# A prefix log-sum-exp over 4096 rows: another order at the end, another split into tiles, and other overflow checks

## The chip, the cores and the metric

The kernel runs on one core of one Trainium2 chip. The metric is the device time of one launch in microseconds. A core has engines that run side by side and wait for each other through semaphores: PE (TensorE, matrix products into PSUM), DVE (VectorE), ACT (ScalarE, here Exp and Ln), POOL (GpSimd) and SP (SyncE, which here only issues transfers), and 16 DMA engines that move data between HBM and the on-chip SBUF.

## The reference

For each of four batches and each of 4128 columns, a running log-sum-exp over 4096 rows:

```
B, S, D = 4, 4096, 4128
out[:, 0, :] = x[:, 0, :]
for t in range(1, S):
    mx = np.maximum(out[:, t - 1, :], x[:, t, :])
    out[:, t, :] = mx + np.log(np.exp(out[:, t - 1, :] - mx) + np.exp(x[:, t, :] - mx))
```

Input and output are float32, 270.5 MB each. Since out[t] is the log of the sum of exp(x) over rows 0 to t, the kernel computes exp, a prefix sum over rows, and a log, without the maximum. Whether that was safe for the data is looked at on the way (the probes, below); if it was not, a slow general routine runs afterwards.

## The kernel before

**Tiles.** A batch's 4096 rows are cut into tiles of 2 or 3 times 128 rows. Partition p of a tile holds r consecutive rows (r is 2 or 3), each of 4128 columns. Every batch is split as 2,3,3,3,2,3,3,3,2,3,3,2, twelve tiles and 48 in all, counted from 0 here. There are four buffers: three of three rows (pool `x3`) and one of two (pool `x2`), which every fourth tile takes. A tile's columns are worked in three chunks of 1376.

**A chunk**, as class `Chunk` has it:

- `exp` (ACT, L92): Exp of all r rows in place.
- `sums` (DVE, L103 for three rows, L105 always): sums within a partition, so that `z` holds each partition's total for partitions 0 to 126. Partition 127 of `z` still holds what the chunk of the same columns in the tile before left there, that is the running total so far.
- `head` (PE, L113): a product of a triangular matrix with `z`, which gives each partition the sum of all rows before it; `carried` also adds the running total, `below` is for a batch's first tile. The result lies in PSUM tile `pt`, of which there are two.
- `add` (DVE, L121 and L122): adds `pt` to all rows but the last, and then writes the last row's sum to `z`, which is the next tile's running total.
- `log` (ACT, L135 and L136): Ln of the rows, the last one from `z`, into the tile.

After its three chunks a tile is stored (SP, L83). Loads are issued at L80. All transfers are issued by SP, in program order.

**Probes.** In a batch's first tile `sums` also takes, per chunk, the minimum over the first row (DVE, L99). In a batch's last tile `add` also takes, per chunk, the sum over columns of the last 32 partitions of `z` (DVE, L128). At the end these are compared with `SMALL` and `LARGE`, and a product on PE makes one flag of them.

**Order.** The kernel switches the scheduler off, so each engine runs its instructions in the order in which the program writes them. One loop runs over all chunks, 144 of them. In each turn it writes the Exp of the chunk two ahead, the sums of the next chunk, then the add and the log of this one, at a tile's end its store and the next load, and the matmul of the next chunk. For the chunks where the one two ahead lies in the last tile, or where there is none, the branch `late` writes the Exp and the sums behind the add and the log instead. The load of tile t+3 stands behind the store of tile t, and waits for the store of tile t-1, whose buffer it takes.

The lines of that branch:

```
        late = far is None or far.t is steps[-1]
        if not late:
            far.exp()
            nxt.sums()
        k.add()
        k.log()
        if late:
            if far:
                far.exp()
            if nxt:
                nxt.sums()
```

Of the kernel before, what the change touches and what calls it, by code (L numbers as in the profile page):

```python
# [7 lines left out]
FP32 = mybir.dt.float32  # L8
I32 = mybir.dt.int32
ACT = mybir.ActivationFunctionType  # L10
ALU = mybir.AluOpType
AX = mybir.AxisListType
P = 128
MM = 512
NC = 3
SMALL = 2.0 ** -63
LARGE = 2.0 ** 62


@with_exitstack  # L20
def kernel(
    ctx: ExitStack,
    tc: tile.TileContext,
    x: bass.AP,
    out: bass.AP,
):
    nc = tc.nc
    B, S, D = x.shape
# [12 lines left out]

    below = consts.tile([P, P], FP32, name="below")
    nc.gpsimd.memset(below, 1.0)  # L43
    nc.gpsimd.affine_select(  # L44
        out=below, in_=below, pattern=[[1, P]], compare_op=ALU.is_ge,
        fill=0.0, base=-1, channel_multiplier=-1,
    )

    carried = consts.tile([P, P], FP32, name="carried")
    nc.gpsimd.affine_select(  # L50
        out=carried, in_=below, pattern=[[0, P]], compare_op=ALU.not_equal,
        fill=1.0, base=-(P - 1), channel_multiplier=1,
    )
    ones = consts.tile([P, 1], FP32, name="ones")
    nc.gpsimd.memset(ones, 1.0)

    probe = consts.tile([P, 2, B * NC], FP32, name="probe")
    nc.gpsimd.memset(probe, 1.0)

    z = [zpool.tile([P, CH], FP32, name=f"z{c}") for c in range(NC)]  # L60
    for t in z:
        nc.gpsimd.memset(t, 0.0)  # L62

    ctx_sched = tc.manual_schedule()
    ctx_sched.__enter__()

    class Step:
        def __init__(self, b, row, r, pool, last):
            self.b, self.row, self.r, self.pool = b, row, r, pool
            self.first, self.last = row == 0, last  # L70

        def dram(self, t):
            rows = t[self.b, self.row:self.row + P * self.r, :]
            return rows.rearrange("(p j) d -> p j d", j=self.r)

        def load(self):
            rows = 2 if self.pool is x2 else 3
            full = self.pool.tile([P, rows, D], FP32, name="xt")
            self.xt = full[:, :self.r, :]
            nc.sync.dma_start(out=self.xt, in_=self.dram(x))  # L80

        def store(self):
            nc.sync.dma_start(out=self.dram(out), in_=self.xt)  # L83

    class Chunk:
        def __init__(self, step, c):
            self.t, self.c, self.z = step, c, z[c]
            self.cols = slice(c * CH, (c + 1) * CH)

        def exp(self):  # L90
            e = self.t.xt[:, :, self.cols]
            nc.scalar.activation(e, e, ACT.Exp)  # L92

        def sums(self):
            t, r = self.t, self.t.r
            e = [t.xt[:, j, self.cols] for j in range(r)]
            if t.first:
                k = t.b * NC + self.c
                nc.vector.tensor_reduce(  # L99
                    out=probe[0:1, 1, k:k + 1], in_=e[0][0:1], op=ALU.min, axis=AX.X,  # L100
                )
            if r == 3:
                nc.vector.tensor_tensor(out=e[1], in0=e[0], in1=e[1], op=ALU.add)  # L103
            n = P - 1
            nc.vector.tensor_tensor(  # L105
                out=self.z[0:n], in0=e[r - 2][0:n], in1=e[r - 1][0:n], op=ALU.add,
            )

        def head(self):
            pt = self.pt = ppool.tile([P, CH], FP32, name="pt")  # L110
            w = below if self.t.first else carried
            for a, b in cuts:
                nc.tensor.matmul(  # L113
                    pt[:, a:b], lhsT=w, rhs=self.z[:, a:b], start=True, stop=True,
                )

        def add(self):
            t, r = self.t, self.t.r
            e = t.xt[:, 0:r - 1, self.cols]
            base = self.pt.unsqueeze(1).to_broadcast([P, r - 1, CH])  # L120
            nc.vector.tensor_tensor(out=e, in0=base, in1=e, op=ALU.add)  # L121
            nc.vector.tensor_tensor(  # L122
                out=self.z, in0=t.xt[:, r - 2, self.cols], in1=t.xt[:, r - 1, self.cols],
                op=ALU.add,
            )
            if t.last:
                k = t.b * NC + self.c
                nc.vector.tensor_reduce(  # L128
                    out=probe[96:P, 0, k:k + 1], in_=self.z[96:P], op=ALU.add, axis=AX.X,
                )  # L130

        def log(self):
            t, r = self.t, self.t.r
            e = t.xt[:, 0:r - 1, self.cols]
            nc.scalar.activation(e, e, ACT.Ln)  # L135
            nc.scalar.activation(t.xt[:, r - 1, self.cols], self.z, ACT.Ln)  # L136

    steps = []
    for b in range(B):
        n = S // P  # L140
        parts = []
        while n:
            r = min(2 if len(parts) % 4 == 0 else 3, n)
            if n - r == 1:
                r = 2
            parts.append(r)
            n -= r
        assert len(parts) % 4 == 0 and min(parts) > 1
        row = 0
        for i, r in enumerate(parts):  # L150
            steps.append(Step(b, row, r, x3 if i % 4 else x2, i + 1 == len(parts)))
            row += P * r
        assert row == S

    chunks = [Chunk(s, c) for s in steps for c in range(NC)]
    bufs, ahead, stored = 4, 3, 0
    for s in steps[:bufs]:
        s.load()
    chunks[0].exp()
    chunks[1].exp()  # L160
    chunks[0].sums()
    chunks[0].head()
    n = len(chunks)
    for g, k in enumerate(chunks):
        nxt = chunks[g + 1] if g + 1 < n else None
        far = chunks[g + 2] if g + 2 < n else None
        late = far is None or far.t is steps[-1]
        if not late:
            far.exp()
            nxt.sums()  # L170
        k.add()
        k.log()
        if late:
            if far:
                far.exp()
            if nxt:
                nxt.sums()
        if k.c == NC - 1:
            k.t.store()
            if bufs <= stored + ahead < len(steps):  # L180
                steps[stored + ahead].load()
            stored += 1
        if nxt:
            nxt.head()


    bad = consts.tile([P, 2, B * NC], FP32, name="bad")
    nc.vector.tensor_scalar(
        out=bad[:, 0, :], in0=probe[:, 0, :], scalar1=LARGE, scalar2=None, op0=ALU.is_le,
    )  # L190
    nc.vector.tensor_scalar(
        out=bad[:, 1, :], in0=probe[:, 1, :], scalar1=SMALL, scalar2=None, op0=ALU.is_ge,
    )
    low = consts.tile([P, 1], FP32, name="low")
    nc.vector.tensor_reduce(  # L195
        out=low, in_=bad.rearrange("p a k -> p (a k)"), op=ALU.min, axis=AX.X,
    )
    good = fpool.tile([1, 1], FP32, name="good")
    nc.tensor.matmul(good, lhsT=low, rhs=ones, start=True, stop=True)  # L199
    flag = consts.tile([1, 1], I32, name="flag")  # L200
    nc.vector.tensor_scalar(  # L201
        out=flag, in0=good, scalar1=float(P), scalar2=None, op0=ALU.is_lt,
    )
    ctx_sched.__exit__(None, None, None)

    wrong = nc.values_load(flag[0:1, 0:1], min_val=0, max_val=1)
    with tc.If(wrong > 0):
        _general(tc, x, out)
# [62 lines left out]
```

## Time and profile before

| What | Value |
|---|---|
| median of three runs | 1296.6 us (1295.03 to 1298.33) |
| the profiled execution: its own time | 1293.67 us |
| its span in the trace | 1291.9 us |
| PE busy | 605.4 us (47%) |
| DVE busy | 996.0 us (77%) |
| ACT busy | 937.3 us (73%) |
| POOL busy | 4.6 us, all of it in the first 5.2 us |
| bytes moved, HBM read and written | 270.53 MB each way, 419 GB/s over the span |
| Exp, L92, three rows or two | 3.63 us or 2.48 us |
| sums, L103 and L105 | 1.59 us each |
| add, L121, three rows or two | 3.02 us or 1.58 us |
| carry, L122 | 1.59 us |
| Ln, L135, three rows or two, and L136 | 2.50 us or 1.35 us, and 1.33 us |
| probes L99 and L128, twelve of each | 1.57 us and 1.58 us |
| load from issue to landing, three rows, two rows | 38.9 us, 33.2 us |
| store from issue to landing, three rows, two rows | 23.8 us, 26.4 us |

The span runs from the first instruction to the end of the last; the time of a run is a little longer. All durations are of the one profiled execution. A transfer is issued long before its bytes move where the queue holds others ahead of it, so its time from issue to landing is mostly waiting in the queue. Matmuls overlap each other, so the busy time of PE is not a sum of work. The chain that ended last is followed back from the last instruction, and says nothing of the transfers that lay beside it.

### The profile page before, as it was taken

What the parts mean: (1) busy time and instruction counts of PE and PEld (TensorE: products, weight loads), DVE (VectorE), ACT (ScalarE), POOL (GpSimd) and SP (SyncE); (2) the same over time, 40 slices, a digit from 0 to 9 for tenths busy, and PEclk for the clock granted to TensorE, in tenths of its full rate; (3) what the DMA queues carried; (4) which work ended last, traced back from release to release, by engine and by line L of the source; (5) the groups of instructions that cost most, each with busy time, mean ns of one, the idle gap of its engine ahead of it and who ended that gap; (6) DMA issues with size and microseconds to landing.
All of it is one profiled execution on the core that took longest, in us unless ns stands there. A gap on an engine that the chain in (4) does not pass through costs nothing. (4 is left out here: it accounts for less than half of the span.)

```text
span 1291.9 us, 3364 instructions
## 1 busy us (share of the span) xinstructions
PE 605.4 (47%) x866; PEld 236.8 (18%) x866; DVE 996.0 (77%) x556; ACT 937.3 (73%) x433; POOL 4.6 (0%) x12
## 2 busy tenths in 40 slices
PE   2554356345555335545534534535534553463432
PEld 1221122112122112112211211211211221121110
DVE  4996798679689579669968957957968976895763
ACT  4996687678589669569669957866858866895761
POOL 1000000000000000000000000000000000000000
PEclk9766666667567667666766766766776666676566
DMA  9999999999999999999999999999999999999964
GB/s 402 423 413 428 433 429 432 436 430 404 438 433 427 439 427 431 435 430 420 423 425 435 439 428 439 428 438 426 415 429 429 435 434 432 434 437 429 433 279 180
DMA packets 13843, 541.28 MB, mean 419 GB/s; under 512 B 1536, under 2 KB 1536, under 8 KB 1536
## 3 DMA queue, kind: packets, MB, share of 16 engines
q1 hardware_dynamic: 13824, 541.07, 97.6%
q8 instruction: 7, 0.11, 0.0%
q14 instruction: 12, 0.10, 0.0%
HBM read 270.53 MB, written 270.53 MB: 419 GB/s over the span
## 5 line engine op out<-in xcount | busy, mean ns | idle before, releaser
L113 PE MATMUL pt<-z,carried 128*128 128x512 f32 (+1 forms) x792 | 557.9, 867 | 613.2 <-DVE z L105 613.2
L92 ACT ACTIVATE xt<-xt 128x4128 f32<-128x4128 f32 (+1 forms) x144 | 467.7, 3249 | 240.3 <-DMA xt<-in_x_dram 240.3
L113 PEld LDWEIGHTS pt<-z,carried 128*128 128x128 f32 x792 | 218.0, 293 | 952.4 <-issue 952.4
L121 DVE TENSOR_TENSOR xt<-pt,xt 128x2752 f32<-128x2752 f32 (+1 forms) x144 | 365.6, 2539 | 20.9 <-PE pt L113 20.9
L135 ACT ACTIVATE xt<-xt 128x2752 f32<-128x2752 f32 (+1 forms) x144 | 303.8, 2109 | 100.3 <-DVE z L122 99.7
L103 DVE TENSOR_TENSOR xt<-xt 128x1376 f32<-128x1376 f32 x96 | 152.3, 1587 | 216.4 <-ACT xt L92 216.3
L105 DVE TENSOR_TENSOR z<-xt 127x1376 f32<-127x1376 f32 x144 | 228.9, 1590 | 17.8 <-ACT xt L92 13.8
L122 DVE TENSOR_TENSOR z<-xt 128x1376 f32<-128x1376 f32 x144 | 229.3, 1593 | 4.9
L136 ACT ACTIVATE xt<-z 128x1376 f32<-128x1376 f32 x144 | 192.0, 1333 | 0.0
L113 PE MATMUL pt<-z,below 128*128 128x512 f32 (+1 forms) x72 | 47.3, 817 | 54.4 <-DVE z L105 54.4
L99 DVE TENSOR_REDUCE probe<-xt 1x1 f32<-1x1376 f32 x12 | 18.9, 1571 | 21.8 <-ACT xt L92 21.7
L113 PEld LDWEIGHTS pt<-z,below 128*128 128x128 f32 x72 | 18.7, 276 | 83.1 <-issue 82.9
L128 DVE TENSOR_REDUCE probe<-z 32x1 f32<-32x1376 f32 x12 | 19.0, 1581 | 0.4
L62 POOL MEMSET z<- 128x1376 f32 x3 | 3.7, 1245 | 0.0
L199 PE MATMUL good<-ones,low 128*1 128x1 f32 x2 | 0.2, 164 | 5.4 <-DVE low L195 5.4
L33 ACT ACT_TABLE_LOAD x1 | 1.3, 1283 | 0.8 <-PEq L255 0.8
L199 PEld LDWEIGHTS good<-ones,low 128*1 128x1 f32 x2 | 0.1, 82 | 6.0 <-DVE low L195 6.0
L201 DVE TENSOR_SCALAR flag<-good 1x1 int32<-1x1 f32 x1 | 0.1, 147 | 0.3 <-PE good L199 0.3
L44 POOL TENSOR_SCALAR_AFFINE_SELECT below<-below 128x128 f32<-128x128 f32 x1 | 0.3, 292 | 0.0
L50 POOL TENSOR_SCALAR_AFFINE_SELECT carried<-below 128x128 f32<-128x128 f32 x1 | 0.3, 292 | 0.0
L195 DVE TENSOR_REDUCE low<-bad 128x1 f32<-128x24 f32 x1 | 0.2, 179 | 0.0
L43 POOL MEMSET below<- 128x128 f32 x1 | 0.2, 204 | 0.3 <-POOLq L255 0.3
(8 smaller groups left out, 1.0 us busy)
## 6 DMA issues: line engine op xcount, KB each, us to landing
xt<-in_x_dram SPq DMA_DIRECT2D x32, 6192.0 KB, 38.9
out_dram<-xt SPq DMA_DIRECT2D x32, 6192.0 KB, 23.8
xt<-in_x_dram SPq DMA_DIRECT2D x16, 4128.0 KB, 33.2
out_dram<-xt SPq DMA_DIRECT2D x16, 4128.0 KB, 26.4
```

The source lines that it names most:

```text
L33: nc.scalar.preload_act_table_set("natural_log_exp_and_others")
L62: nc.gpsimd.memset(t, 0.0)
L92: nc.scalar.activation(e, e, ACT.Exp)
L99: nc.vector.tensor_reduce(out=probe[0:1, 1, k:k + 1], in_=e[0][0:1], op=ALU.min, axis=AX.X,)
L103: nc.vector.tensor_tensor(out=e[1], in0=e[0], in1=e[1], op=ALU.add)
L105: nc.vector.tensor_tensor(out=self.z[0:n], in0=e[r - 2][0:n], in1=e[r - 1][0:n], op=ALU.add,)
L113: nc.tensor.matmul(pt[:, a:b], lhsT=w, rhs=self.z[:, a:b], start=True, stop=True,)
L121: nc.vector.tensor_tensor(out=e, in0=base, in1=e, op=ALU.add)
L122: nc.vector.tensor_tensor(out=self.z, in0=t.xt[:, r - 2, self.cols], in1=t.xt[:, r - 1, self.cols], op=ALU.add,)
L128: nc.vector.tensor_reduce(out=probe[96:P, 0, k:k + 1], in_=self.z[96:P], op=ALU.add, axis=AX.X,)
L135: nc.scalar.activation(e, e, ACT.Ln)
L136: nc.scalar.activation(t.xt[:, r - 1, self.cols], self.z, ACT.Ln)
```

## The change

Five things are changed together.

- The branch `late` is gone. Each engine now has a list of its own (`act`, `vec`, `pe` and `moves`), written out for all tiles in one pattern. The pattern is the one that the loop before had away from its end: on ACT, Exp runs two chunks ahead; on DVE, the sums of the next chunk come before the add of this one. A loop then writes the lists out, each as far as what it needs has been written.
- The split into tiles is given as lists: `usual` for the first three batches, `final` for the last one, which now has thirteen tiles, 49 in all. Tiles 45 to 48 have 3, 3, 3 and 2 rows.
- The load of the last tile is issued directly behind the load before it, and so ahead of the store of tile 45 and not behind it.
- The look at a batch's first row is done by GpSimd: a comparison with `SMALL` into `ample` and a product into `least`, per chunk, written behind the chunk's Exp. One DVE minimum over `least` is left for the end.
- The look at a batch's last rows is no instruction of its own: the addition that writes `z` is done by `tensor_tensor_reduce`, which also writes the sum over columns, now for all 128 partitions.

```
--- before.py
+++ after.py
-    probe = consts.tile([P, 2, B * NC], FP32, name="probe")
+    probe = consts.tile([P, B * NC], FP32, name="probe")
     nc.gpsimd.memset(probe, 1.0)
+    least = consts.tile([1, CH], FP32, name="least")
+    nc.gpsimd.memset(least, 1.0)
+    ample = consts.tile([1, CH], FP32, name="ample")
...
         def exp(self):
-            e = self.t.xt[:, :, self.cols]
+            t = self.t
+            e = t.xt[:, :, self.cols]
             nc.scalar.activation(e, e, ACT.Exp)
+            if t.first:
+                nc.gpsimd.tensor_scalar(
+                    out=ample, in0=t.xt[0:1, 0, self.cols], scalar1=SMALL, scalar2=None,
+                    op0=ALU.is_ge,
+                )
+                nc.gpsimd.tensor_tensor(out=least, in0=least, in1=ample, op=ALU.mult)
 
         def sums(self):
-            t, r = self.t, self.t.r
-            e = [t.xt[:, j, self.cols] for j in range(r)]
-            if t.first:
-                k = t.b * NC + self.c
-                nc.vector.tensor_reduce(
-                    out=probe[0:1, 1, k:k + 1], in_=e[0][0:1], op=ALU.min, axis=AX.X,
-                )
...
         def add(self):
...
-            nc.vector.tensor_tensor(
-                out=self.z, in0=t.xt[:, r - 2, self.cols], in1=t.xt[:, r - 1, self.cols],
-                op=ALU.add,
-            )
+            ends = (t.xt[:, r - 2, self.cols], t.xt[:, r - 1, self.cols])
             if t.last:
-                k = t.b * NC + self.c
-                nc.vector.tensor_reduce(
-                    out=probe[96:P, 0, k:k + 1], in_=self.z[96:P], op=ALU.add, axis=AX.X,
+                nc.vector.tensor_tensor_reduce(
+                    out=self.z, in0=ends[0], in1=ends[1], scale=1.0, scalar=0.0,
+                    op0=ALU.add, op1=ALU.add, accum_out=probe[:, k:k + 1],
                 )
+            else:
+                nc.vector.tensor_tensor(out=self.z, in0=ends[0], in1=ends[1], op=ALU.add)
...
+    usual = [2, 3, 3, 3, 2, 3, 2, 3, 2, 3, 3, 3]
+    final = [2, 3, 2, 3, 2, 2, 3, 2, 2, 3, 3, 3, 2]
...
+    moves = [("load", t) for t in range(SLOTS)]
+    ahead = SLOTS
+    for t in range(n):
+        moves.append(("store", t))
+        if t and ahead < n:
+            moves.append(("load", ahead))
+            ahead += 1
+            if ahead == n - 1:
+                moves.append(("load", ahead))
+                ahead += 1
...
+    act.append(("exp", 0, 0))
+    act.append(("exp", 0, 1))
+    vec.append(("sums", 0, 0))
+    for t in range(n):
+        act += [("exp", t, 2), ("log", t, 0), ("exp", t + 1, 0), ("log", t, 1),
+                ("exp", t + 1, 1), ("log", t, 2)]
+        vec += [("sums", t, 1), ("add", t, 0), ("sums", t, 2), ("add", t, 1),
+                ("sums", t + 1, 0), ("add", t, 2)]
+        pe += [("head", t, c) for c in range(NC)]
...
+    fits = consts.tile([P, B * NC + 1], FP32, name="fits")
+    nc.vector.memset(fits[:, B * NC:], 1.0)
+    nc.vector.tensor_reduce(
+        out=fits[0:1, B * NC:], in_=least, op=ALU.min, axis=AX.X,
+    )
```

Of the old code, the loop over chunks with its branch `late` and the rule that split the batches are taken out; the two comparisons with `SMALL` and `LARGE` at the end become one with `LARGE`, over `probe`.

More of the change, by code (lines that the diff above doesn't have):

```diff
@@ L15 @@
 NC = 3
+SLOTS = 4
 SMALL = 2.0 ** -63
@@ L90, in exp @@
         def exp(self):
-            e = self.t.xt[:, :, self.cols]
+            t = self.t
+            e = t.xt[:, :, self.cols]
             nc.scalar.activation(e, e, ACT.Exp)
-        def sums(self):
-            t, r = self.t, self.t.r
-            e = [t.xt[:, j, self.cols] for j in range(r)]
-            if t.first:
-                k = t.b * NC + self.c
-                nc.vector.tensor_reduce(
-                    out=probe[0:1, 1, k:k + 1], in_=e[0][0:1], op=ALU.min, axis=AX.X,
-                )
+            if t.first:
[4 more added lines that the diff above has]
+                nc.gpsimd.tensor_tensor(out=least, in0=least, in1=ample, op=ALU.mult)
+        def sums(self):
+            r = self.t.r
+            e = [self.t.xt[:, j, self.cols] for j in range(r)]
             if r == 3:
@@ L118, in add @@
             t, r = self.t, self.t.r
+            k = t.b * NC + self.c
             e = t.xt[:, 0:r - 1, self.cols]
@@ L136, in log @@
             nc.scalar.activation(t.xt[:, r - 1, self.cols], self.z, ACT.Ln)
+    usual = [2, 3, 3, 3, 2, 3, 2, 3, 2, 3, 3, 3]
+    final = [2, 3, 2, 3, 2, 2, 3, 2, 2, 3, 3, 3, 2]
     steps = []
     for b in range(B):
[L140 to L148, printed above, removed]
+        parts = final if b == B - 1 else usual
@@ L149 @@
         row = 0
         for i, r in enumerate(parts):
-            steps.append(Step(b, row, r, x3 if i % 4 else x2, i + 1 == len(parts)))
+            if row == S:
+                break
+            pool = x3 if len(steps) % SLOTS else x2
+            steps.append(Step(b, row, r, pool, row + P * r == S))
             row += P * r
         assert row == S
[L155 to L184, printed above, removed]
@@ L187 @@
-    bad = consts.tile([P, 2, B * NC], FP32, name="bad")
-    nc.vector.tensor_scalar(
-        out=bad[:, 0, :], in0=probe[:, 0, :], scalar1=LARGE, scalar2=None, op0=ALU.is_le,
+    for s in steps:
+        s.chunks = [Chunk(s, c) for c in range(NC)]
+    n = len(steps)
+    moves = [("load", t) for t in range(SLOTS)]
[8 more added lines that the diff above has]
+                ahead += 1
@@ new lines @@
+    lists = {"move": moves, "act": [], "vec": [], "pe": []}
+    act, vec, pe = lists["act"], lists["vec"], lists["pe"]
+    act.append(("exp", 0, 0))
[7 more added lines that the diff above has]
+        pe += [("head", t, c) for c in range(NC)]
@@ new lines, in needs @@
+    def needs(what, t, c=None):
+        if what == "load":
+            return [("store", t - SLOTS)]
+        if what == "store":
+            return [("log", t, c) for c in range(NC)]
+        return {
+            "exp": [("load", t)],
+            "sums": [("exp", t, c), ("log", t - 1, c)],
+            "head": [("sums", t, c), ("add", t - 1, c)],
+            "add": [("head", t, c)],
+            "log": [("add", t, c)],
+        }[what]
+    done, at = set(), {e: 0 for e in lists}
+    while any(at[e] < len(l) for e, l in lists.items()):
+        before = len(done), sum(at.values())
+        for e, l in lists.items():
+            while at[e] < len(l):
+                op = l[at[e]]
+                if op[1] < n:
+                    if any(0 <= d[1] and d not in done for d in needs(*op)):
+                        break
+                    done.add(op)
+                    of = steps[op[1]]
+                    getattr(of if len(op) == 2 else of.chunks[op[2]], op[0])()
+                at[e] += 1
+        assert before != (len(done), sum(at.values()))
@@ L190 @@
+    fits = consts.tile([P, B * NC + 1], FP32, name="fits")
+    nc.vector.memset(fits[:, B * NC:], 1.0)
+    nc.vector.tensor_reduce(
+        out=fits[0:1, B * NC:], in_=least, op=ALU.min, axis=AX.X,
     )
     nc.vector.tensor_scalar(
-        out=bad[:, 1, :], in0=probe[:, 1, :], scalar1=SMALL, scalar2=None, op0=ALU.is_ge,
+        out=fits[:, :B * NC], in0=probe, scalar1=LARGE, scalar2=None, op0=ALU.is_le,
     )
     low = consts.tile([P, 1], FP32, name="low")
-    nc.vector.tensor_reduce(
-        out=low, in_=bad.rearrange("p a k -> p (a k)"), op=ALU.min, axis=AX.X,
-    )
+    nc.vector.tensor_reduce(out=low, in_=fits, op=ALU.min, axis=AX.X)
```

## The prediction

> **What bounds the kernel now.** I read the slices of the page first, then its DMA queues, then windows over the end, then the issues of SP, and the chain that ended last only after these.
>
> ```profile
> DMA  9999999999999999999999999999999999999964
> GB/s 402 423 413 428 433 429 432 436 430 404 438 433 427 439 427 431 435 430 420 423 425 435 439 428 439 428 438 426 415 429 429 435 434 432 434 437 429 433 279 180
> q1 hardware_dynamic: 13824, 541.07, 97.6%
> ```
>
> The reader sees that the transfers fill 38 of 40 slices and that only the last two sag. DVE is busy for 77% of the span and ACT for 73%: neither sets the time in the middle, they run ahead of the loads (ACT waited 240.3 us for loads in the table of waits). So the time is bytes over rate, plus whatever the queue stands dry. Windows of ten microseconds over the end (columns: stretch, length, busy time and count of PE, PEld, DVE, ACT, POOL, granted clock, DMA share, GB/s):
>
> ```profile
> 1230.00:1240.00 10.00, 4.93 (x6) 1.86 (x6) 4.85 (x4) 6.35 (x4) 0.00 (x0) 0.54 0.78 337
> 1240.00:1250.00 10.00, 3.86 (x5) 1.83 (x6) 5.96 (x3) 5.42 (x3) 0.00 (x0) 0.50 0.19 79
> 1250.00:1260.00 10.00, 3.36 (x5) 1.20 (x5) 6.36 (x4) 5.68 (x4) 0.00 (x0) 0.67 0.92 396
> 1260.00:1270.00 10.00, 3.36 (x6) 1.39 (x5) 6.36 (x4) 2.59 (x2) 0.00 (x0) 0.67 0.37 159
> 1270.00:1280.00 10.00, 2.94 (x7) 1.00 (x6) 5.34 (x7) 2.59 (x2) 0.00 (x0) 0.67 0.12 53
> 1280.00:1290.00 10.00, 0.00 (x0) 0.00 (x0) 0.00 (x0) 0.00 (x0) 0.00 (x0) 0.50 0.87 371
> ```
>
> What is missing to a share of 1 in these six is 2.2 + 8.1 + 0.8 + 6.3 + 8.8 + 1.3 = 27.5 us. That is the idle that a change of the end can win. Why it is there is seen in the issues of the last three stores (tiles 45, 46, 47, counted from 0) and in one load that landed before them:
>
> ```profile
> 1207.25 3.64 ACT L92 ACTIVATE xt<-xt 128x4128 f32<-128x4128 f32 x1 [7.69 <-DMA xt<-in_x_dram]
> 1222.56 0.33 SPq L83 DMA_DIRECT2D out_dram<-xt  x1
> 1248.34 0.33 SPq L83 DMA_DIRECT2D out_dram<-xt  x1
> 1278.72 0.33 SPq L83 DMA_DIRECT2D out_dram<-xt  x1
> ```
>
> A tile of three rows is 6192 KB, which at the steady 433 GB/s is 14.6 us (estimate), one of two rows 9.8 us. Store 45 is through 15 us after 1222.56, store 46 is issued 26 us after it and store 47 another 30 us later: twice the queue waits for compute. The chain says on what:
>
> ```profile
> 1257.70 4.42 PE pt L113 x6
> 1262.12 0.02 issue
> 1262.14 1.60 DVE xt L121
> 1263.75 0.02 issue
> 1263.77 1.60 DVE z L122
> 1265.38 0.02 issue
> 1265.40 1.58 DVE probe L128
> 1266.98 0.03 issue
> 1267.01 1.60 DVE z L105
> 1268.62 0.14 issue
> 1268.75 4.02 PE pt L113 x6
> ```
>
> In the last tile each chunk runs alone: matmul, add, carry, probe, then the sums of the next chunk, and only then its matmul: 11 us a chunk, 33 us for a tile whose DVE work, spread as in the middle, takes half of that.
>
> **The change, part by part.**
>
> Order kept to the end. The branch `late` goes, so the sums of the next chunk stand before the add of this one in the last tile too, and its matmul lies beside that add. Cost per chunk from the rows: exp 3.63 or 2.48 (three or two rows), sums 3.2 or 1.6, add with carry 3.02 + 1.59 = 4.6 or 1.6 + 1.6 = 3.2, Ln pair 3.8 or 2.7, matmul 4 to 4.9. Check on the middle: from the landing of a load to the issue of the store of the tile before lie exp, sums, add and Ln pair, 3.6 + 3.2 + 4.6 + 3.8 = 15.2; the lines above show 1222.56 - 1207.25 = 15.3.
>
> New end, 3,3,3,2 (tiles 45 to 48), and load 48 ahead of store 45. Put T at the landing of load 47. Behind it the one queue then holds load 48 (9.8), stores 45, 46 and 47 (14.6 each) and store 48 (9.8): it is busy to T + 63.4 if each is issued in time. Store 46 is issued at T + 15.3; the queue needs it at T + 24.4. From there DVE sets the pace, its last add of tile 46 being done at T + 11.4: sums 14.6, add 19.2, sums 22.4, add 27.0, sums of tile 48 28.6, add 33.2, Ln pair: store 47 at T + 37.1, needed at T + 39.0. Tile 48: sums 34.8, add 38.0, sums 39.6, matmul of chunk 1 from 34.9 to 39.9, add 43.1, matmul of chunk 2 to 44.8, add 48.0, Ln pair: store 48 at T + 50.7, needed at T + 53.6. So nothing runs dry, with 2 to 3 us to spare, and all 27.5 us go. An issue takes one to two microseconds to become bytes (load 0: issue 0.81, share 0.72 in the first five), so the two tight stores may leave 0 to 4 us; I take 1. The shares are means over 16 engines and the last one counts; the share falls from 0.92 to 0.18 at 1238 and to 0 at 1240, so I add 2 (0 to 3).
>
> Thirteen tiles. The old split 3,3,2 under the new order would leave store 46 due at 15.3 + 21.8 = 37 us after the landing of load 46, with 9.8 + 9.8 + 14.6 = 34 us queued: some 4 us dry. The new split is worth that, inside the 27.5. The bytes are the same; two more transfers, three more chunks on PE and nine more ACT instructions lie under DMA.
>
> Load 48 before store 45. SP stands at this load until store 44 has landed, and store 45 is behind it. Store 44 lands 9.8 us after load 46, store 45 has its data only at 15.3: nothing waits. The transfer merely trades places with a store: 0.
>
> Split in the middle. Between the landing of load t+1 and the end of load t+2 the queue holds store t-1 and load t+2. The old split has one place a batch with two rows on both (4 rows, 19.5 us, against the 15.3 needed; tile 9: 262.86 to 278.18); `usual` has 5 or 6 rows everywhere. `final` has 4 at tiles 39, 41 and 42, where a two-row tile shortens the need to 12.7 (measured at 1178.02 to 1190.74). No new dry place; the old one shows no dip in the windows around 278 (0.95, 0.99, 0.94), so I take 0, at best -3.
>
> Probes. The first-row reductions (12 x 1.571) and the last-row ones (12 x 1.581) leave DVE, 37.9 us, hidden under DMA in the middle. In the last tile the 1.58 per chunk leaves the chain, already left out above. In its place a sum rides on the carry, with a second small instruction that reads it out. No row shows it: between 1.59 (L122 alone) and 3.17 (L122 and L128), plus 0.15 (the flag instruction). I take 1.6 + 0.15, the same stream over the same two operands as L122; at the upper end, with the read-outs, store 48 moves to about T + 54.5, or 2 us late with its start, which lies in the 0 to 4. [...]
>
> GpSimd. It gets 24 instructions on 1x1376, two per chunk of a batch's first tile. Nearest rows:
>
> ```profile
> L62 POOL MEMSET z<- 128x1376 f32 x3 | 3.7, 1245 | 0.0
> L44 POOL TENSOR_SCALAR_AFFINE_SELECT below<-below 128x128 f32<-128x128 f32 x1 | 0.3, 292 | 0.0
> ```
>
> That gives 1.25 us each at the low end and 292 / 128 x 1376 = 3.1 at the high one. The select reads as well as writes and so is nearest; less the 0.1 of an empty instruction it gives 2.2, or 4.4 a pair. The new wait: the add of such a chunk must not overwrite rows that GpSimd still reads. In the first tile the third look ends at 31.3 even at 3.1 each (start 15.8, five instructions), and that add stood at 35.9, about 32.8 without two probes before it: covered, by 1.5 us at the worst. Stores do not wait for GpSimd. I take 0, from -1 (store 1 was issued at 66.05, about when store 0 ended; 3.1 us less DVE before it) to the rival below. The closing look at the flag gains one 1.57 reduction, under the 9.8 us of the last store.
>
> Sum on the profiled run: span 1291.9 - 27.5 + 1 + 2 = 1267.4, its time 1293.67 - 24.5 = 1269.2. The median of the three runs lies 2.9 above that run: 1272.
>
> **The rivals.**
>
> GpSimd holds DVE up. If a look and a DVE instruction with both operands in SBUF can't run together, each batch start costs DVE up to three pairs. At the first batch DVE is busy without a gap from 23 to 66 and store 1 has no slack, so the loss is 3p - 3.1 for a pair of p. At the three others the queue has 24.4 - 15.3 = 9.1 in hand and DVE is relieved of 4.7 there: 3p - 13.8. With p = 4.4 that is 10 us, all at the start: 1282. For it: nothing shows the two engines together (POOL works only in the first 5 us). Against it: the adds, the longest DVE work, take one operand from PSUM, and the looks last 13 us while the first tile waits for its matmuls anyway. [...]
>
> The same at a higher price, which is the case on the other side: the four batch starts together lose 12p - 44.5, which passes the 24.5 won at p = 5.75, or 2.9 us a look. At the high row, p = 6.2, it is 30 us: 1302, slower. It needs the high row and every look blocking in full.
>
> The end stays bound by compute. If stores 47 and 48 miss by more than I reckon (the carry with its sum at 3.2, matmuls at 4.9 throughout, a Ln pair late behind an exp), the queue is dry for 4 to 8 us more: 1276 to 1280. For it: the spare time is 2 to 3 us in 50. Against it: the check of 15.3 fits to 0.1.
>
> The change does not do what it says: four stores in a row don't run at the mixed rate, and the end gains less. The lone store at 1250 to 1260 moved at 396 with a share of 0.92, which is 430 at a full share: little room for it. At 10% less over the 54 us of stores it would be +5: 1277.
>
> **How the numbers follow.** Forecast 0.76, with its own range 1266 to 1276; GpSimd at a middle price 0.10 (1276 to 1290); a late end or slow stores 0.07 (1276 to 1282); slower through GpSimd 0.04; no net change, by several of these prices together, 0.03. The range must leave out no more than 2 in 10: 1265 (27.5 less, 3 more in the middle, 1 at the start) to 1284, which takes in the GpSimd rival at its middle price. About 0.3%, 4 us, is what a measurement here can tell from no change: faster 0.93, same 0.03, slower 0.04.
>
> **What would show it.** The last two slices of the page at 400 GB/s or more; the last four stores issued while the one before is still moving, and the span ending 10 to 13 us after the last issue; windows over the last 60 us with shares of 0.9 and more. The chain that ended last has no probe and no chunk of 11 us. DVE busy some 35 us lower. The carry with its sum at 1.6 (or 3.2), the looks at 2.2 (or otherwise), and in the first 70 us no DVE instruction longer than in the profile before. It is wrong if store 1 is issued after 68 us, if stores 47 or 48 come more than 4 us after the queue emptied, or if the middle slices fall below 420.

## The result, and the profile after

The changed kernel takes 1275.4 us (median of four runs, 1274.7 to 1276.4) against 1296.9: a ratio of 0.9836, interval 0.9819 to 0.9853. The forecast was 1272, in 1265 to 1284. Its profiled run took 1275.27 us with a span of 1273.6, which is 18.3 less than the span before. The profiled run before (1293.67) was about 3 us faster than its median, so spans show a smaller gain than medians.

The slices of the page (40 of 31.8 us) and the row of its DMA queue:

```profile
GB/s 407 420 318 422 425 437 429 434 431 426 439 433 427 431 433 429 438 430 437 431 430 433 431 433 432 433 433 429 434 440 425 439 429 435 425 411 415 429 442 345
q1 hardware_dynamic: 14112, 541.07, 98.9%
```

The sag of the last two slices (279 and 180 before) is gone but for a rest in the very last. A new one has come: slice 3, about 64 to 96 us, is down to 318.

Windows over the end, the same view as before:

```profile
1240.00:1250.00 10.00, 5.92 (x11) 2.31 (x10) 8.44 (x7) 9.99 (x6) 0.00 (x0) 0.80 0.79 342
1250.00:1260.00 10.00, 2.01 (x7) 0.66 (x5) 7.31 (x11) 5.18 (x4) 0.00 (x0) 0.72 0.93 401
1260.00:1270.00 10.00, 0.00 (x0) 0.00 (x0) 0.00 (x0) 0.00 (x0) 0.00 (x0) 0.50 0.98 421
1270.00:1273.60 3.60, 0.00 (x0) 0.00 (x0) 0.00 (x0) 0.00 (x0) 0.00 (x0) 0.50 0.02 9
```

The last two columns are the DMA share and GB/s. Only 2.1 + 0.7 + 0.2 + 3.5 = 6.5 us are missing here, of which 1.9 stood behind the last bytes before the change too. So about 23 of the 27.5 us are won. (A packet counts in the window in which it begins; that is why a share can pass 1, and a short window is rough.) The first Exp on load 47, which begins as that load lands, and the issues of the last three stores:

```profile
1208.38 3.65 ACT L97 ACTIVATE xt<-xt 128x4128 f32<-128x4128 f32 x1 [1.45 <-DMA xt<-in_x_dram]
1223.70 0.34 SPq L87 DMA_DIRECT2D out_dram<-xt  x1
1245.14 0.33 SPq L87 DMA_DIRECT2D out_dram<-xt  x1
1258.12 0.33 SPq L87 DMA_DIRECT2D out_dram<-xt  x1
```

From T = 1208.4 store 46 comes at T + 15.3, store 47 at T + 36.8 and store 48 at T + 49.7; the walk had 15.3, 37.1 and 50.7.

The start, windows of two microseconds in the new sag:

```profile
66.00:68.00 2.00, 2.00 (x4) 0.86 (x3) 2.00 (x1) 2.00 (x2) 0.00 (x0) 0.62 0.20 83
68.00:70.00 2.00, 1.86 (x3) 0.34 (x1) 1.97 (x2) 1.79 (x1) 0.00 (x0) 0.53 0.00 0
70.00:72.00 2.00, 0.00 (x0) 0.00 (x0) 1.97 (x3) 1.80 (x1) 0.00 (x0) 1.00 0.00 0
72.00:74.00 2.00, 0.61 (x1) 0.50 (x2) 2.00 (x2) 2.00 (x3) 0.00 (x0) 0.83 0.00 0
```

Store 0 is through at 67 us, store 1 is issued at 73.97 (66.05 before), and for close to 8 us no byte moves. DVE (the third column behind the width) is busy throughout these windows. Why it is late stands in the timeline of the first tile:

```profile
15.82 3.68 POOL L99 TENSOR_SCALAR ample<-xt 1x1376 f32<-1x1376 f32 x1 [9.43 <-ACT xt L97]
15.83 8.90 DVE L111 TENSOR_TENSOR z<-xt 127x1376 f32<-127x1376 f32 x2 [15.83 <-ACT xt L97]
19.58 3.70 POOL L103 TENSOR_TENSOR least<-least,ample 1x1376 f32<-1x1376 f32 x1
...
25.44 1.59 DVE L128 TENSOR_TENSOR xt<-pt,xt 128x1376 f32<-128x1376 f32 x1 [0.71 <-PE pt L119]
...
28.36 3.70 POOL L103 TENSOR_TENSOR least<-least,ample 1x1376 f32<-1x1376 f32 x1
29.04 4.47 DVE L111 TENSOR_TENSOR z<-xt 127x1376 f32<-127x1376 f32 x1
```

Two sums take 8.90 us where they took 3.2, the next 4.47, while GpSimd has its looks beside them. Taken together, DVE instructions are longer by 13.3 us at this first batch start, and by 8.3 at each of the three later ones. The add (L128), whose one operand is in PSUM, keeps its 1.59 beside a comparison (23.37 to 28.27). Over the whole run (line, engine, operation, shapes, count, busy time, mean ns, idle before):

```profile
L111 DVE TENSOR_TENSOR z<-xt 127x1376 f32<-127x1376 f32 x147 | 259.8, 1768 | 58.2 <-ACT xt L97 54.6
L99 POOL TENSOR_SCALAR ample<-xt 1x1376 f32<-1x1376 f32 x12 | 57.9, 4827 | 855.8 <-ACT xt L97 855.1
L103 POOL TENSOR_TENSOR least<-least,ample 1x1376 f32<-1x1376 f32 x12 | 45.0, 3750 | 1.0
L131 DVE CUSTOM_DVE_ANT_0 z<-xt 128x1376 f32<-128x1376 f32 x12 | 19.1, 1592 | 0.4
L131 DVE DVE_READ_ACCUMULATOR2_ANT probe<- 128x1 f32 x12 | 1.0, 83 | 0.0
```

A look is a comparison of 4.83 us and a product of 3.75 us, 8.6 a pair, twice what was taken. All 147 sums together have a mean of 1.768 for the 1.59 of an undisturbed one. The carry with its sum takes 1.592 + 0.083.

### The profile page after: what moved, and what is told of

Its sections match the earlier page's. It is cut to its first block, busy times and chain, and to the rows that moved or that the text cites. A ratio compares the mean times of both kernels' runs of the same rounds, so it can differ in the third digit from the quotient of the medians.

```text
span 1273.6 us, 3466 instructions
## 1 busy us (share of the span) xinstructions
PE 609.9 (48%) x884; PEld 237.6 (19%) x884; DVE 993.9 (78%) x548; ACT 938.3 (74%) x442; POOL 108.7 (9%) x37
## 3 DMA queue, kind: packets, MB, share of 16 engines
q1 hardware_dynamic: 14112, 541.07, 98.9%
## 4 chain that ended last, share of the span: by engine, by line
DMA 66%; DVE 19%; ACT 12%; issue 1%; PE 1%; SPq 0%; ACTq 0%; DVEq 0%
DMA xt<-in_x_dram 54%; DMA out_dram<-xt 13%; DVE xt L128 7%; ACT xt L97 5%; DVE z L111 5%; ACT xt L141 4%; DVE z L136 3%; DVE xt L109 3%; ACT xt L142 2%; PE pt L119 1%; DVE z L131 0%; SPq L87 0%; ACTq L141 0%; ACTq L97 0%; SPq L84 0%
## 5 line engine op out<-in xcount | busy, mean ns | idle before, releaser
L128 DVE TENSOR_TENSOR xt<-pt,xt 128x2752 f32<-128x2752 f32 (+1 forms) x147 | 361.8, 2461 | 0.7 <-PE pt L119 0.7
L111 DVE TENSOR_TENSOR z<-xt 127x1376 f32<-127x1376 f32 x147 | 259.8, 1768 | 58.2 <-ACT xt L97 54.6
L109 DVE TENSOR_TENSOR xt<-xt 128x1376 f32<-128x1376 f32 x90 | 145.7, 1619 | 199.5 <-ACT xt L97 199.5
L136 DVE TENSOR_TENSOR z<-xt 128x1376 f32<-128x1376 f32 x135 | 224.2, 1660 | 4.6
L142 ACT ACTIVATE xt<-z 128x1376 f32<-128x1376 f32 x147 | 196.3, 1335 | 0.0
L99 POOL TENSOR_SCALAR ample<-xt 1x1376 f32<-1x1376 f32 x12 | 57.9, 4827 | 855.8 <-ACT xt L97 855.1
L119 PE MATMUL pt<-z,below 128*128 128x512 f32 (+1 forms) x72 | 52.4, 895 | 60.6 <-DVE z L111 60.6
L103 POOL TENSOR_TENSOR least<-least,ample 1x1376 f32<-1x1376 f32 x12 | 45.0, 3750 | 1.0
L131 DVE CUSTOM_DVE_ANT_0 z<-xt 128x1376 f32<-128x1376 f32 x12 | 19.1, 1592 | 0.4
## 6 DMA issues: line engine op xcount, KB each, us to landing
out_dram<-xt SPq DMA_DIRECT2D x19, 4128.0 KB, 21.5
```

The source lines that it names most:

```text
L99: nc.gpsimd.tensor_scalar(out=ample, in0=t.xt[0:1, 0, self.cols], scalar1=SMALL, scalar2=None, op0=ALU.is_ge,)
L103: nc.gpsimd.tensor_tensor(out=least, in0=least, in1=ample, op=ALU.mult)
L111: nc.vector.tensor_tensor(out=self.z[0:n], in0=e[r - 2][0:n], in1=e[r - 1][0:n], op=ALU.add,)
L119: nc.tensor.matmul(pt[:, a:b], lhsT=w, rhs=self.z[:, a:b], start=True, stop=True,)
L131: nc.vector.tensor_tensor_reduce(out=self.z, in0=ends[0], in1=ends[1], scale=1.0, scalar=0.0, op0=ALU.add, op1=ALU.add, accum_out=probe[:, ...
L136: nc.vector.tensor_tensor(out=self.z, in0=ends[0], in1=ends[1], op=ALU.add)
```

## The experiments

The theory after this reading: the new order gives most of the gain; GpSimd's looks hold DVE up and cost 8 us at the start and nothing later; the new split gives some 4 us; the early last load and the merged sum give nothing. The rivals stand in each expectation. All times are medians of four or more runs, with the ratio to the kernel before on the same chip.

### The changed kernel again, beside three ways to look at the first rows

> The changed kernel itself, to stand beside the three others on one chip. Both theories: ratio to the kernel before 0.984, about 1275.5 us at a before of 1297; store 1 issued at 74 us, with the queue dry from about 67 to 75.

Measured: 1276.4 us, ratio 0.9843 (0.9826 to 0.9859), store 1 at 73.93.

The look back on DVE:

```
-            if t.first:
-                nc.gpsimd.tensor_scalar(out=ample, in0=t.xt[0:1, 0, self.cols], ...)
-                nc.gpsimd.tensor_tensor(out=least, in0=least, in1=ample, op=ALU.mult)
...
         def sums(self):
+            if self.t.first:
+                nc.vector.tensor_reduce(
+                    out=first[:, k:k + 1], in_=e[0][0:1], op=ALU.min, axis=AX.X,
+                )
```

> The changed kernel with the first-row look back on DVE, one reduction of 1.57 us per chunk before the sums; all else as changed. Theory (GpSimd's looks hold DVE up at the start and that alone costs the 8 us that the queue stands dry there): store 1 at about 66 us as in the kernel before, the sums of the first tile back from 4.5 to 1.59 us, 7 to 8 us faster than the changed kernel, about 1268. Rival (the start is late for another reason, or the lateness is given back later under the slack of the queue): the same 1275 or, with the reductions added to DVE, slower.

Measured: 1268.2 us, ratio 0.9782 (0.9766 to 0.9798), 8.2 us faster than the changed kernel. Windows from 60 to 80 us, first of this kernel and then, in a fence of its own, of the changed one:

```profile
60.00:70.00 10.00, 6.27 (x10) 2.02 (x8) 9.90 (x7) 9.17 (x5) 0.00 (x0) 0.69 0.99 429
70.00:80.00 10.00, 4.24 (x6) 1.65 (x6) 9.90 (x6) 9.58 (x5) 0.00 (x0) 0.82 1.08 451
```

```profile
60.00:70.00 10.00, 7.09 (x11) 2.35 (x9) 9.90 (x6) 9.38 (x4) 0.00 (x0) 0.68 0.64 277
70.00:80.00 10.00, 4.20 (x6) 1.70 (x6) 9.90 (x7) 9.38 (x4) 0.00 (x0) 0.83 0.56 238
```

The dry stretch is the whole difference: 0.36 and 0.44 of ten microseconds are 8.0. Store 1 is issued at 65.75.

No look at all (the six lines taken out of `exp`; the first rows are then not checked):

> The changed kernel without any look at the first rows (that check is left out of the computation). Theory: store 1 at about 63 us, no dry queue at the start, DVE busy 38 us less than in the changed kernel (what its instructions were stretched by), time 0 to 1 us under that of the look on DVE, about 1267. Rival: 1275.

Measured: 1266.7 us, ratio 0.9772 (0.9756 to 0.9789). Store 1 comes at 65.07, two microseconds later than expected: without the reductions the first tile waits for its matmuls instead (DVE's idle before the adds of two rows, ended by PE, is 4.6 us over the run and 1.2 with the reductions on DVE). DVE is busy 956.2 us, 37.7 less than in the changed kernel. So of 103 us of looks 38 went into longer DVE instructions.

A look that needs neither engine for long:

```
+    firsts = consts.tile([P, W], FP32, name="firsts")      # W = B * D // P = 129
...
+    for b in range(B):
+        nc.sync.dma_start(out=firsts[b * n_b:(b + 1) * n_b],
+            in_=x[b, 0:1, :].rearrange("o (p d) -> (o p) d", d=W))
...
+    nc.vector.tensor_reduce(out=fits[:, B * NC:], in_=firsts, op=ALU.min, axis=AX.X)
+    nc.vector.tensor_scalar(out=fits[:, B * NC:], in0=fits[:, B * NC:], scalar1=LOWEST,
+        scalar2=None, op0=ALU.is_ge)
```

> The changed kernel with the first rows of the four batches fetched once more by four small loads (66 KB in all, issued behind the first four tiles) and looked at once, by one DVE minimum at the end, with x itself compared with the log of the bound. Theory: as without any look, plus the small transfers, 0.2 us by their bytes and up to 2 us if small pieces are slow: 1267 to 1269, faster than both kernels. Rival: 1275.

Measured: 1264.3 us, ratio 0.9752 (0.9736 to 0.9768): faster than both kernels, and a little below the range expected. Its queue is at work in 99.6% of the span, against 98.9% in the changed kernel.

### Does GpSimd hold DVE up by being there, or by reading?

```
             if t.first:
-                nc.gpsimd.tensor_scalar(out=ample, in0=t.xt[0:1, 0, self.cols], ...)
-                nc.gpsimd.tensor_tensor(out=least, in0=least, in1=ample, op=ALU.mult)
+                for _ in range(7):
+                    nc.gpsimd.memset(spare, 1.0)
```

> The changed kernel with the looks replaced by 84 memsets of 1x1376 on GpSimd (about 104 us of work that only writes; the check of the first rows is left out); they wait for nothing, so they run in one piece from about 6 to 110 us. Theory (the two engines exclude each other where a GpSimd instruction reads SBUF and DVE reads two operands there): DVE's sums and carries stay at 1.59 us beside them, store 1 at about 63 us, 1267. Rival (any GpSimd work slows DVE): sums of 3 us and more until 110 us, store 1 at 75 us or later, 1275 or slower.

Measured: 1266.7 us, ratio 0.9768 (0.9744 to 0.9792), as without any look. The timeline of the first tile, and the group of memsets over the run:

```profile
12.80 28.37 POOL L100 MEMSET spare<- 1x1376 f32 x22
15.79 1.59 DVE L108 TENSOR_TENSOR z<-xt 127x1376 f32<-127x1376 f32 x1 [15.79 <-ACT xt L97]
```

```profile
L100 POOL MEMSET spare<- 1x1376 f32 x84 | 103.7, 1235 | 4.8
```

As much GpSimd work as the looks were (103.7 us against 102.9), and the sums stay at 1.59. In these runs DVE is held up beside the looks, which read SBUF, and not beside the memsets, which only write: a sum takes 4.47 us beside the one and 1.59 beside the other. What grew, the sums and carries, reads both operands in SBUF. The adds, with one operand in PSUM, never grew: in the changed kernel they take 1.58 and 1.59 us beside a comparison (at 33.43 and 25.44), and over the run 1.583 for two rows and 3.018 for three, where the kernel before has 1.582 and 3.018. It is not a matter of a shared tile: the product reads only `least` and `ample`, which DVE does not touch then, and the sums beside it took 4.47. But the memsets differ from the looks in their kind of operation as well as in not reading, and no run here separates the two.

How long a sum is held up beside a look can be read from the ends. In the first tile of the changed kernel the product begun at 28.36 ends at 32.06 and the sums beside it, begun at 29.04, at 33.51, 1.45 us later and nearly a whole 1.59. Beside a comparison the distance is shorter:

```profile
32.15 4.90 POOL L99 TENSOR_SCALAR ample<-xt 1x1376 f32<-1x1376 f32 x1
...
35.05 2.84 DVE L136 TENSOR_TENSOR z<-xt 128x1376 f32<-128x1376 f32 x1
```

Here the ends are 37.05 and 37.89, 0.84 us apart. Both distances come again at the second batch's start (1.45 and 0.84). If DVE runs at its usual pace once a look has ended, an estimate that no run isolates, it stands still for nearly the whole product and for all but some 0.75 us of a comparison (1.59 - 0.84); whether that rest is overlap, or the roughness of GpSimd's spans, stays open.

### The looks alone, on the kernel before

The same six lines in `exp` of the kernel before, and its L99 taken out of `sums`; one minimum over `least` stands at the end.

> The kernel before with the looks on GpSimd and nothing else changed. Theory: store 1 at 74 us, queue dry for 8 us there, the rest hidden: 7 to 8 us slower, about 1304. Rival (the lateness is made good later): 1297.

Measured: 1303.3 us, ratio 1.0053 (1.0036 to 1.0070): 7.5 us slower, store 1 at 74.05. By itself this part of the change is a loss; it came in beside a larger gain.

### The order alone, and the order taken back

On the kernel before:

```
-        late = far is None or far.t is steps[-1]
+        late = False
         if not late:
-            far.exp()
-            nxt.sums()
+            if far:
+                far.exp()
+            if nxt:
+                nxt.sums()
```

> The kernel before with the order kept to the end and nothing else changed. Theory: the last store 17 to 20 us sooner, about 1278; of the 27.5 us idle at the end 4 to 8 are left, since store 46 is not in time. Rival (the gain is the split's): 1290 or more.

Measured: 1277.3 us, ratio 0.9856 (0.9827 to 0.9885), 18.5 us less than before. The issues of its last two stores, 46 and 47 (48 tiles with the old split, 49 with the new), and the window in which store 46 falls:

```profile
1247.22 0.33 SPq L83 DMA_DIRECT2D out_dram<-xt  x1
1262.21 0.33 SPq L83 DMA_DIRECT2D out_dram<-xt  x1
```

```profile
1240.00:1250.00 10.00, 6.42 (x12) 2.34 (x10) 9.68 (x7) 10.00 (x6) 0.00 (x0) 0.78 0.35 149
```

Store 47 now follows 15 us behind store 46 and not 30. Store 46 is still late: with a share of 0.35, 6.5 us are missing in its window.

In the changed kernel, with the branch put back for the last two tiles:

```
+        if t == n - 2:
+            act += [("exp", t, 2), ("log", t, 0), ("log", t, 1), ("exp", t + 1, 0),
+                    ("log", t, 2), ("exp", t + 1, 1)]
+            vec += [("sums", t, 1), ("add", t, 0), ("add", t, 1), ("sums", t, 2),
+                    ("add", t, 2), ("sums", t + 1, 0)]
+        elif t == n - 1:
+            act += [("log", t, 0), ("exp", t, 2), ("log", t, 1), ("log", t, 2)]
+            vec += [("add", t, 0), ("sums", t, 1), ("add", t, 1), ("sums", t, 2),
+                    ("add", t, 2)]
```

> The changed kernel with the order of the branch late put back for the last two tiles, on DVE and ACT; split, load order and probes as changed. Theory (the order is most of the gain): chunks of the last tile 9 to 10 us apart again, store 48 some 16 us later, about 1290. Rival (the new split alone keeps the queue fed): 1276 to 1279.

Measured: 1293.1 us, ratio 0.9976 (0.9964 to 0.9988), 16.7 us slower than the changed kernel. Its chain that ended last has the chunks by themselves again:

```profile
1256.81 4.70 PE pt L119 x6
...
1261.53 1.60 DVE xt L128
...
1263.15 1.59 DVE z L131
...
1264.75 1.51 DVE z L111
...
1266.40 4.94 PE pt L119 x6
```

9.6 us a chunk (11 before, less the 1.58 of the probe), and store 48 at 1277.30, 27 us behind store 47 at 1250.05. Some 17 of the changed kernel's 21 us hang on this order, and the split cannot stand in for it.

### The split

`usual` and `final` both set to 2,3,3,3,2,3,3,3,2,3,3,2 in the changed kernel.

> The changed kernel with the old split 2,3,3,3,2,3,3,3,2,3,3,2 in every batch, 48 tiles. Theory: at the end store 46 comes 4 us after the queue emptied, and the three places in the middle where four rows are queued leave early DMA engines dry for about 1.5 us: 4 to 6 us slower than the changed kernel, about 1280. Rival (the split is worth nothing once the order is kept): 1275.

Measured: 1287.4 us, ratio 0.9928 (0.9902 to 0.9954): 11 us slower than the changed kernel, twice what was expected. The order alone with all looks on DVE (1277.3) against the changed kernel with its look on DVE (1268.2) gives 9.1 for the split, the merged sum and the early load together. The GB/s of their pages, first of the order alone and then of the changed kernel with the look on DVE:

```profile
GB/s 406 418 411 426 433 434 437 429 433 408 432 430 431 432 436 420 441 434 411 414 438 434 431 427 432 430 437 429 419 411 437 434 436 427 431 428 441 425 382 332
```

```profile
GB/s 409 415 417 431 432 423 437 430 439 433 427 434 431 429 439 426 439 429 434 433 434 429 432 443 424 432 431 435 434 438 428 438 423 417 432 404 431 422 436 350
```

With the old split there are low slices after each batch's end: 408, then 411 and 414, then 419 and 411, in slices of 31.9 us. Against 433 that is 1.8 + 3.0 + 2.7 = 7.5 us of mean transfer, and the last two slices lose some more. The new split has low places of its own in the last batch, 417 in slice 34 and 404 in slice 36, where store 42 came late (issued at 1115.99; from 1114 to 1118 about 1.1 us of transfer are missing), so the net is smaller than 7.5.

How much belongs to the middle and how much to the end can be read from the DMA packets of the traces, by the time at which the same number of bytes has been moved (541 MB in all). The order alone is behind the changed kernel with its look on DVE by 0.2 us at 100 MB, 8.6 at 450 MB (after the three batch ends), only 3.6 at 500 MB, where the new split has paid for its own low places, and 9.4 at the end of the span. The old split in the changed kernel is behind the changed kernel by 0.7, 9.5, 4.9 and 11.6 at the same marks. So the three batch ends are worth some 9 us in these two pairs, the new split gives back some 5 of them in the last batch, and the end is worth some 6. The kernel before, which has the old split as well, is 6.3 us behind the changed kernel with its look on DVE at 450 MB: single traces with the old split differ by 2 us there, so 6 to 9 is as close as this comes.

One more split, with the small load: `final = [2, 2, 2, 3, 2, 3, 2, 3, 2, 3, 3, 3, 2]`.

> The kernel with the small load, and in the last batch the split 2,2,2,3,2,3,2,3,2,3,3,3,2: the queue then holds 5 or 6 rows at every tile but one (tile 38), where the split of the changed kernel has 4 at tiles 39, 41 and 42 and store 41 is issued 1 us after the first DMA engine ran dry. Theory (a dry place costs even the slowest engine 1 to 2 us, because the transfer behind it takes that much longer): no late store near 1110 us, 1 to 3 us faster than with the small load alone, 1262 to 1263. Rival (only the early engines wait, the slowest sets the end): the same 1264.

The late store that the expectation calls 41 is store 42, counted from 0 (1112.52 with the small load).

Measured: 1262.4 us, ratio 0.9739 (0.9725 to 0.9754). Slices 31 to 39 of its page lie at 428 GB/s or more, where the small load alone has 415 and 418 among them. In the two traces it is 1.9 us ahead at 500 MB, but only 0.9 at the end of the span. Next to 0.9752 for the small load alone, 1.9 us is what the theory expected, but the two intervals overlap: probable, not shown. It is the fastest kernel of the study, 2.6% below the one before.

### The two parts costed at nothing

The last load in its usual place (the three lines from `if ahead == n - 1` on taken out):

> The changed kernel with the last load in the usual place, behind store 45. Theory: the transfer trades places with a store and nothing waits for it: within 1.5 us of the changed kernel, 1274 to 1277. Rival (the early load feeds the end): 4 us or more slower.

Measured: 1276.3 us, ratio 0.9848 (0.9827 to 0.9870). No difference.

The sum over the last rows as a reduction of its own:

```
-                nc.vector.tensor_tensor_reduce(out=self.z, in0=ends[0], in1=ends[1], ...)
+                nc.vector.tensor_tensor(out=self.z, in0=ends[0], in1=ends[1], op=ALU.add)
+                nc.vector.tensor_reduce(
+                    out=probe[96:P, k:k + 1], in_=self.z[96:P], op=ALU.add, axis=AX.X,
+                )
```

> The changed kernel with the last-row sum as a reduction of its own, 1.58 us behind each carry of a batch's last tile, over the last 32 partitions as in the kernel before. Theory: store 48 is issued 2 to 3 us later, at about T + 52.5, still before store 47 has ended on the slowest engine: 0 to 1.5 us slower, 1275 to 1277. Rival (the chain of the last tile sets the end): 3 x 1.6 us slower, 1280.

Measured: 1276.5 us, ratio 0.9844 (0.9822 to 0.9865). No difference. The last store does come later, at 1261.20 against 1259.38 in the repeated changed kernel, but store 47 (1246.22 and 1246.42) keeps the queue at work nearly until then: the 1.58 per chunk still delays the last store, and no longer the end.

## Why the prediction was right, and where its terms were off

**The end.** Right in place and size. 27.5 us of idle was the whole to be won, and about 23 of it went. The walk from T came out to 1 us at each of three stores. Its spare time was what was wrong. Store 47 was to have 1.9 us in hand, the queue lasting to T + 39.0 = 1247.4, but with each packet spread over its own time the queue ran empty from about 1243.6 (a share of 0.33 from 1243.5 to 1244.0), 1.5 us before the store was issued at 1245.14. The windows show the hole more roughly:

```profile
1242.00:1244.00 2.00, 0.79 (x2) 0.49 (x3) 2.00 (x2) 2.00 (x2) 0.00 (x0) 1.00 0.29 124
1244.00:1246.00 2.00, 2.00 (x4) 0.75 (x3) 1.97 (x2) 2.00 (x2) 0.00 (x0) 0.52 0.35 149
1246.00:1248.00 2.00, 1.29 (x3) 0.25 (x1) 0.66 (x3) 2.00 (x2) 0.00 (x0) 0.63 1.50 644
```

With the time that the issue took to become bytes (0.9 us: by the same packets the share is 0.07 in the half microsecond before 1246.0 and 0.93 in the one after), about 2 us were lost. From T to 1243.6 are 35.2 us, 15.2 MB at 433 GB/s, where the walk has 16.9 MB (two stores of three rows and load 48). That part of load 48 was already through when the last bytes of load 47 landed is the likely reason, which no run isolates. The terms "I take 1" for the two tight stores and "I add 2" for uneven engines were large enough to cover it, though neither was worked out from this.

**The order.** It was to bring most of the 27.5 us, all but the split's 4 and the 3 that were to stay, so some 20; alone it gives 18.5.

**Thirteen tiles and the middle.** The terms "some 4 us dry" for the old end and "0, at best -3" for the middle were too small: 9 to 11 together, some 6 of it at the end and the rest in the middle (6 to 9 won at the batch ends, 5 lost again in the last batch). The step that failed is the reading of the windows around 278. They show no dip in the share of busy DMA engines; what falls is the rate, later: from 290 to 310 the kernel before has shares of 1.04 and 1.00 with 414 and 396 GB/s.

```profile
290.00:300.00 10.00, 4.86 (x10) 2.07 (x11) 9.74 (x6) 10.00 (x6) 0.00 (x0) 0.94 1.04 414
300.00:310.00 10.00, 6.35 (x9) 2.18 (x7) 8.52 (x6) 6.47 (x4) 0.00 (x0) 0.54 1.00 396
```

These are the kernel before's own windows. Busy engines that move less than 433 count as full in a share. With each packet spread over its own time, the trace does have a small dip at the place with four rows queued, 0.4 us from 278 to 280; about 15 and 25 us behind it follow two stretches (292 to 298, 302 to 306) in which all engines are busy at 312 to 406 GB/s. Together they lack 2.2 us of transfer, and the order alone, with the same split, is 2.3 us behind the changed kernel with its look on DVE at 130 MB, just past this batch end. So the 4 us in hand (19.5 against 15.3) were not enough to keep every engine fed. Why the later transfers are slower no run shows. Nor was "no new dry place" right: store 42 is one.

**GpSimd.** The term "I take 0" was wrong by 8 us, and it is the first rival that happened, at the place it named (store 1, with no slack in hand) and near the price it gave (10). That the price came near is luck: its working was off twice, in opposite directions. The pair cost 8.6 us and not 4.4: neither the memset nor the select was a good row for a comparison or product on one partition. And a look does not hold DVE for all its length: 38 of 103 us did. So the threshold of 5.75 us a pair, above which the kernel was to be slower, is refuted: at 8.6 it is 21 us faster. At the three later batch starts 8.3 us of holding up each fitted into the 13.8 that the queue had in hand; no such slack stood behind the 13.3 at the first.

**The merged sum.** Taken at 1.6 + 0.15, measured at 1.592 + 0.083 in the changed kernel's 12 instructions (`CUSTOM_DVE_ANT_0` in the trace) that add two float32 operands from SBUF and accumulate. The upper end of what was reckoned with, 3.17, did not show there.

**The early load.** Costed at nothing, and nothing it is.

**The signs.** By its own list the prediction was wrong about the start: store 1 was issued at 73.97 and not before 68, a DVE instruction of the first 70 us took 4.47 us, and DVE was busy for 993.9 us (996.0 before) and not 35 less. Slices 36 and 37 are under 420 (411 and 415), the last slice is at 345, and the span ends 15.5 us after the last issue and not 10 to 13. The signs for the order held: the last stores follow each other closely, and the chain that ended last has no chunk of 11 us.

So 27.5 - 3 was forecast; 8 were lost at the start, part of it made up by a split worth more than reckoned, and 21.5 remain. Set beside the kernel before by bytes moved, the changed kernel (profiled runs) is 7.6 us behind at 100 MB, 1.6 at 450 MB, 6.1 at 500 MB, and 18.3 ahead at the end. The gain at the end is what was forecast. That the total came within 4 us of the forecast is in part luck: of two terms taken at nothing, one lost 8 us and the other won some 2 to 5, so that they offset each other in part.

## What to carry to other kernels

In a kernel that is full of transfers, look for the few places where the queue runs dry (the start, the end, and wherever the rows queued last little longer than the compute between two issues), and read GB/s beside the share of busy engines. Cheap work moved to an idle engine is not free because that engine was idle: here GpSimd's looks, which read SBUF, stretched DVE's sums of two SBUF operands from 1.59 us to as much as 4.51, and by themselves made the kernel 7.5 us slower. So move such work where DVE has slack, or fetch the few bytes again in a shape that takes one short instruction (0.28 us on 128x129). A large gain in one place hides a loss in another; taking the parts apart one by one, and replacing the one that lost, gave a kernel 13 us faster than the change as made.

## What the runs showed that was not expected

- A GpSimd comparison on one partition of 1376 float32 elements takes 4.83 us and a product 3.75, with DVE at work beside them, where a memset of the same shape takes 1.235.
- With the old split a carry merged with its sum takes 1.904 us in the mean and not 1.592. That a batch's last tile overlaps the next batch's looks there is the likely reason, which no run isolates.
- The four small loads of 66 KB in all cost nothing that the median shows: the kernel with them is not slower than the one without any look (0.9752 against 0.9772). The 2 us that the expectation allowed for slow small pieces were the author's estimate, and no run shows them.
